# Gather conditions kept to one engine, and the tables of extra blocks moved into the first expert of a mixture-of-experts kernel

## The chip, the cores and the metric

The kernel runs on one core of one Trainium2 chip. The metric is the device time of one launch in microseconds. The kernel before takes 1557.82 us, the median of three runs (1555.93 to 1558.26).

Five engines work side by side, each with its own queue of instructions: PE (TensorE, matrix products), DVE (VectorE), ACT (ScalarE), POOL (GpSimd) and SP (SyncE, which here does little but issue transfers). Waits between them are semaphores. An engine's queue is in order: whatever stands behind a waiting instruction waits too.

## The reference

One decoder block over 512 tokens of width 1024, and after it a mixture of experts. The experts are where the change lies, so only they are shown:

```
def moe(h, router_w, router_b, w_in, b_in, w_out, b_out):
    logits = (tok @ router_w + router_b)            # tok: 512 x 1024, 32 experts
    top_val, top_idx = lax.top_k(logits, TOP_K)     # TOP_K = 4
    weights = jax.nn.softmax(top_val, axis=-1)
    ...                                             # tokens sorted by expert, padded to blocks
    def expert_block(args):
        rows, e = args
        xb = tok[rows]
        gu = xb @ w_in[e] + b_in[e]                 # 1024 x 2048
        gate, up = gu[:, :D_EXPERT], gu[:, D_EXPERT:]
        gate = jnp.minimum(gate, SWIGLU_LIMIT)
        up = jnp.clip(up, -SWIGLU_LIMIT, SWIGLU_LIMIT)
        act = (up + 1) * (gate * jax.nn.sigmoid(SWIGLU_ALPHA * gate))
        return act @ w_out[e] + b_out[e]            # 1024 x 1024
    ...                                             # weighted, added to the token's row
x = x + gate2[:, None, :] * moe(h, ...)
return rms_norm(x, final_g)
```

All weights are fp32: 12 MB for each of the 32 experts.

## The kernel before, in words

**Stages.** Up to about 400 us of the profile run the front of the block, the router and the tables that say which token goes into which slot. From 421.7 us to about 1522 us the 32 experts run one after the other. A last norm ends the kernel.

**Slots.** Each expert has a main block of slots (`ab_up` L1298, `ab_down` L1313). Where an expert got more tokens, a *single* block and a *pair* block are computed as well, each under a condition at run time: `tc.If(single[e] > 0)` and `tc.If(pair[e] > 0)`, in L1414 and L1416 for the first product ("up") and in L1437 and L1439 for the second ("down"). The up conditions stand ahead of the main `ab_up`. A condition is a branch on every engine that has work in it, and its false path still brings the semaphores to the count that the block would have left, so that others can wait on plain numbers. The two flags of an expert are loaded into a register of each engine by `values_load` in `gather_first`.

**Gathers.** POOL gathers the rows of a block from DRAM (`gather`, L1241). The gathers of single and pair blocks stand under two more conditions (L1254, L1256), which before are branches on all five engines though only POOL has work in them. They run two experts ahead.

**Tables.** `tables` (L1184) makes from sums of slots the rows to gather. The table of main blocks (`tab0`) is made in the router. Those of single and pair blocks (`tab1`, `tabp`) are made by `later_tables(1)` ahead of expert 0: 16 products with one-hots (`spread`, L1112), a copy by ACT (`slt`), five products with `reps` (L1192) and eleven operations of DVE. Then comes a condition on `most` (L1396) for the tables of the seventh block on, which is false with these inputs.

**Weights.** Each expert has 12 tiles of 1 MB: eight `wi` (L937) and four `wo` (L942). SP issues them ahead through `prefetch`. They lie in a ring of 19 places (`big`, tag "H"). Two of these are held by the one-hots `oh` and by `rx` until the tables are made. I number the tiles W0 to W11 (expert 0), W12 to W23 (expert 1) and so on. W12 to W15 go into places that are free by then. W16 goes into the place of W0, which is expert 0's `wi[0]`, W17 into that of W1, and so on: a tile is issued when the last instruction of the program that reads its predecessor is done, whether that stands in a condition or not.

**Order.** PE's order is the order in which the code is written (`manual_schedule`); the other engines' is set by the scheduler of the framework. In `ab_up` 30 of 32 products run (60 of 64 rows of the profile, which shows each as two), then `between()` (here `before_last`: `swiglu` of the first half, its transposes, the biases of the second product), then the last four. In `ab_out` `halfway` prepares the next expert's rows.

Of the kernel before, what the change touches and what calls it, by code (L numbers as in the profile page):

```python
# [9 lines left out]
F32 = mybir.dt.float32  # L10
# [31 lines left out]
def tile_hybrid_block(ctx: ExitStack, tc: tile.TileContext, x, c, ada_w, ada_b, norm1_g, w_in,  # L42
# [1049 lines left out]
    def one_hots(p_, n, i):  # L1092

        ns = slice(4 * i, 4 * i + 4)
        return v.tensor_tensor(oh[:, ns, 0:n], iota_l[:, 0:n].unsqueeze(1).to_broadcast([128, 4, n]),
                               p_[:, ns].unsqueeze(2).to_broadcast([128, 4, n]), op=OP.is_equal)
# [13 lines left out]
    def spread(t, n, i):  # L1110
        for k in range(4 * i, 4 * i + 4):
            pe.matmul(t[0:n, 0:96], oh[:, k, 0:n], rv[:, k].rearrange("p a e -> p (a e)"),  # L1112
                      start=(k == 0), stop=(k == 15))
# [15 lines left out]
    oh = H([128, 16, 128], F32R, name="oh")  # L1129
    slot_ps = M()  # L1130
# [54 lines left out]
    def tables(t, n, reps, tab, mul, o, ps_, tile_):  # L1185

        N = tab.shape[1]
        r = tile_("slt")[0:n]
        sc.activation(r, t[0:n, 0:96], AF.Copy)
        ps = ps_()  # L1190
        for b, rep in enumerate(reps):
            pe.matmul(ps[:, 96 * b:96 * b + 96], rep[0:n], r, start=True, stop=True)  # L1192
        pv = ps[:, 0:96 * N].rearrange("p (n v e) -> p n v e", n=N, v=3)
        iv, em = [tile_(n).rearrange("p (n e) -> p n e", e=32)[:, 0:N] for n in ("iv", "em")]
# [11 lines left out]
    tables(slot_ps, 64, rep64, tab0, 2.0, 2, M, front_tile)  # L1206
# [38 lines left out]
    single, pair = {}, {}  # L1245

    def gather_first(e):
        single[e], pair[e] = [nc.values_load(nbt[0:1, o + e:o + e + 1], min_val=0, max_val=1) for o in (32, 64)]  # L1248
# [110 lines left out]
    for t in xab[1:] + xce:  # L1359
        gp.memset(t, 0.0)  # L1360

# [12 lines left out]
    def later_tables(ch):  # L1374
# [6 lines left out]
        s_ = rows_of(0) if ch == 1 else None  # L1381
        tab = mo.tile([128, 512], F32, tag="yab", bufs=2, name="tl")[:, 0:384].bitcast(I32) if ch > 1 else None
        tab = tab.rearrange("p (n e w) -> p n e w", n=4, w=3) if ch > 1 else tab1
        tables(t, 128, rep32, tab, 4.0, 0, PT, mo_tile)
        if ch == 1:
            tables(t, 64, rep64, tabp, 2.0, 2, PT, mo_tile)
            v.copy_predicated(tab1[:, 0], pair4.unsqueeze(2).to_broadcast([128, 32, 3]), tab1[:, 2])
        gp.dma_start(tabl[4 * ch - 2:4 * ch + 2].rearrange("n p f -> p n f"), tab.rearrange("p n e w -> p n (e w)"))
        return s_
# [16 lines left out]
    def expert(e, xT, sel, p):  # L1406
        (wi, wo), n = W[e], e // 16
        x_ = xce[e % 3]
        if e + 2 < NE:
            gather_first(e + 2)  # L1410
            gather_more(e + 2)
        sel1 = selectors(e + 1) if e + 1 < NE else None
        act, last = acts(2, "act"), acts(3, "actc")
        with tc.If(single[e] > 0):  # L1414
            c_up(transposed(x_[:, 512:768], 2, "xc", 2, True), wi, sel, n, last[2])
        with tc.If(pair[e] > 0):  # L1416
            pp = [PC(), PC()]
            xp = transposed(x_[:, 0:512], 4, "xab", 2, True)
            ab_up(xp, wi, up_biases(sel, n, pp))
            for t, a_ in zip(pp, last):  # L1420
                swiglu(t, a_)
# [14 lines left out]
        swiglu(p[1], act[1])  # L1436
        with tc.If(single[e] > 0):  # L1437
# [38 lines left out]

    with tc.If(most > 5):
# [91 lines left out]
```

## Time and profile before

| | us |
|---|---|
| median of three runs | 1557.82 |
| the profiled execution's own time | 1551.44 |
| its span (first to last instruction) | 1549.9 |
| PE busy in it | 1388.0 (90%) |
| time before and behind the span | 1.5 |

The profile is one execution, 6.4 us below the median. In the rows, "x" is a count, times are from the span's start, and what stands in brackets is the idle time of the engine just before, with what ended it. PEq, SPq and DVEq are the sequencers of these engines: time that went into branches, loads of registers or semaphores.

### The profile page before, as it was taken

To read this page: it belongs to the slowest core of one execution; us is meant where nothing else is said; L and a number is where in the kernel's file an instruction comes from. 1 tells how busy PE (TensorE), PEld (TensorE's weight loads), DVE (VectorE), ACT (ScalarE), POOL (GpSimd) and SP (SyncE) were. 2 spreads that over 40 slices of the span, in tenths; PEclk is the share of its full clock that TensorE was granted. 3 is DMA by queue.
4 is the path that set the end of the run, shared out by engine and by line. 5 is a ranking of instruction groups with operands and counts; after the bars stand their busy time and mean duration, and the time that the engine had idled before them with its cause. 6 is when DMAs were issued, how large, how long until landed. Compare 5 with 4: busy or idle time off the path is not lost. (4 is left out here: it accounts for less than half of the span.)

```text
span 1549.9 us, 22296 instructions
## 1 busy us (share of the span) xinstructions
PE 1388.0 (90%) x7895; PEld 673.5 (43%) x7896; DVE 451.5 (29%) x1089; ACT 346.1 (22%) x830; POOL 220.4 (14%) x181
## 2 busy tenths in 40 slices
PE   5759999999588889999999999999999999998992
PEld 4548877778433333333333333333333333333330
DVE  7558932474411111111111111112112111111113
ACT  3452333334211211121120111111121111221112
POOL 3733100000200110111010110111101111110001
PEclk9879999999599999999999999999999999999997
DMA  9424576594799999999997899999999999678953
GB/s 313 135 63 136 214 256 179 170 342 156 286 391 407 410 405 404 405 407 400 408 402 280 330 398 409 406 353 398 402 409 372 399 411 405 246 292 332 388 181 131
DMA packets 128918, 497.11 MB, mean 321 GB/s; under 512 B 23588, under 2 KB 31236, under 8 KB 95972
## 3 DMA queue, kind: packets, MB, share of 16 engines
q1 hardware_dynamic: 113844, 468.50, 77.2%
q0 software_dynamic: 11888, 20.84, 5.9%
q10 hardware_dynamic: 3008, 5.38, 1.0%
q8 instruction: 114, 1.87, 0.5%
q14 instruction: 64, 0.52, 0.1%
HBM read 476.75 MB, written 20.40 MB: 321 GB/s over the span
## 5 line engine op out<-in xcount | busy, mean ns | idle before, releaser
L1304 PE MATMUL pu<-wi,xab 128*64 128x512 f32 x2048 | 463.0, 604 | 42.2 <-PEq L1416 33.2
L1304 PEld LDWEIGHTS pu<-wi,xab 128*64 128x64 f32 x2048 | 165.1, 139 | 315.3 <-issue 304.5
L1317 PE MATMUL pd<-wo,aab 128*64 128x512 f32 x1024 | 234.6, 598 | 16.9 <-PEq L1439 15.5
L1279 ACT ACTIVATE s<-g 128x256 f32<-128x256 f32 x88 | 36.6, 416 | 679.8 <-DVE g L1278 669.1
L1317 PEld LDWEIGHTS pd<-wo,aab 128*64 128x64 f32 x1024 | 74.5, 137 | 155.8 <-issue 141.3
L1278 DVE TENSOR_SCALAR g<-pu 128x256 f32<-128x256 f32 x64 | 27.0, 421 | 354.0 <-PE pu L1304 353.7
L1270 ACT ACTIVATE xab<-pt,sh2c,g2c 128x64 f32<-128x64 f32 x304 | 93.8, 413 | 11.1 <-PE pt L1264 9.4
L1338 PE MATMUL pc<-wi,xc 128*32 128x512 f32 x768 | 85.1, 594 | 3.1 <-ACT xc L1270 2.9
L1304 PE MATMUL pc<-wi,xab 128*64 128x512 f32 x384 | 83.9, 594 | 2.2 <-DMA wi<-in_moe_w_in 1.3
L1326 DVE SCALAR_TENSOR_TENSOR yab<-pd,tab,gate2h 128x512 f32<-128x512 f32 x32 | 24.0, 751 | 200.4 <-PE pd L1317 200.4
L1241 POOL DMA_INDIRECT xab<-hrow,tab x32 | 34.2, 1070 | 327.7 <-PE pt L1264 325.6
L1355 POOL DMA_INDIRECT acc<-yab,tab x32 | 51.1, 1597 | 159.4 <-DVE yab L1326 71.1
L1355 POOL DMA_INDIRECT acc<-yc,tab x12 | 19.9, 1657 | 350.8 <-DVEq L1439 232.8
L174 ACT ACTIVATE whi<-wraw 128x1024 fp32r<-128x1024 f32 x46 | 48.2, 1056 | 90.5 <-PE g L386 65.0
L386 PE MATMUL g<-hhi,whi 128*128 128x512 f32 x160 | 64.6, 404 | 1.8 <-ACT hhi L498 1.8
L386 PE MATMUL g<-hlo,whi 128*128 128x512 f32 x160 | 63.8, 399 | 1.5 <-DVE hlo L492 1.4
L386 PE MATMUL g<-hhi,wlo 128*128 128x512 f32 x160 | 63.5, 397 | 0.0
L1272 ACT ACTIVATE aab<-pt 128x256 f32<-128x256 f32 x64 | 24.5, 383 | 149.2 <-PE pt L1264 149.2
L1278 DVE TENSOR_SCALAR g<-pc 128x256 f32<-128x256 f32 x24 | 10.2, 424 | 162.4 <-PE pc L1338 86.7
L175 POOL TENSOR_TENSOR wlo<-wraw,whi 128x1024 fp32r<-128x1024 f32 x16 | 40.5, 2535 | 89.5 <-ACT whi L174 89.0
L1304 PEld LDWEIGHTS pc<-wi,xab 128*64 128x64 f32 x384 | 27.3, 137 | 56.2 <-issue 50.9
L1338 PEld LDWEIGHTS pc<-wi,xc 128*32 128x32 f32 x768 | 23.6, 110 | 57.4 <-issue 40.1
(442 smaller groups left out, 1616.4 us busy)
## 6 DMA issues: line engine op xcount, KB each, us to landing
wi<-in_moe_w_in SPq DMA_DIRECT2D x256, 1024.0 KB, 17.0
wo<-in_moe_w_out SPq DMA_DIRECT2D x128, 1024.0 KB, 14.2
adaw<-in_ada_w SPq DMA_DIRECT2D x16, 1024.0 KB, 5.2
wraw<-in_w_in SPq DMA_DIRECT2D x12, 1024.0 KB, 7.4
wraw<-in_ada_w SPq DMA_DIRECT2D x8, 1024.0 KB, 9.3
wraw<-in_w_out SPq DMA_DIRECT2D x4, 1024.0 KB, 9.8
xt<-in_x SPq DMA_DIRECT2D x4, 512.0 KB, 5.3
wraw<-in_w_in SPq DMA_DIRECT2D x4, 512.0 KB, 13.4
```

Of the source, the lines that this page charges most:

```text
L174: sc.activation(dst_hi, src, AF.Copy)
L175: lo.tensor_sub(dst_lo, src, dst_hi)
L386: pe.matmul(P["ps"][m], l, r, start=(k == 0 and n == 0), stop=(k == 2 * P["n"] - 1 and n == 2))
L1241: gp.indirect_dma_start(out=dst, out_offset=None, in_=rows_, in_offset=bass.IndirectOffsetOnAxis(ap=idx, axis=0), bounds_check=n * S - 1, ...
L1270: sc.activation(t[:, o:o + w], ps[:, o:o + w], AF.Identity, scale=g2c[:, k:k + 1], bias=sh2c[:, k:k + 1])
L1272: sc.activation(t, ps[:, 0:128 * n], AF.Copy)
L1278: v.tensor_scalar(g, p[:, 0:256], LIMIT, None, op0=OP.min)
L1279: sc.activation(sg, g, AF.Sigmoid, scale=ALPHA)
L1304: pe.matmul(p[u][64 * g:64 * g + 64, :].rearrange("p (a b) -> p a b", a=2), xT[:, k % 4, 64 * (k // 4):64 * (k // 4) + 64], wi[k][:, :, 51 ...
L1317: pe.matmul(p[64 * g:64 * g + 64, :], aT[:, k % 2, 16 * (k - k % 4):16 * (k - k % 4) + 64], wo[k // 2 + j][:, k % 2, 512 * g:512 * g + 512 ...
L1338: pe.matmul(p[32 * g:32 * g + 32, :].rearrange("p (a b) -> p a b", a=2), xT[:, k % 2, 32 * (k // 2):32 * (k // 2) + 32], wi[k][:, :, 256 * ...
L1355: gp.indirect_dma_start(out=rows_, out_offset=bass.IndirectOffsetOnAxis(ap=icol, axis=0), in_=y, in_offset=None, compute_op=OP.add)
```

## The change

- The flags of an expert are loaded twice: for POOL alone in `gather_more`, and for PE, DVE, ACT and POOL in `halfway` of the expert before (for expert 0 ahead of it). The gather conditions are branches of POOL alone; SP, PE, ACT and DVE keep an unconditional branch for each. SP loads no flags.
- `later_tables` is split: `later_sums` (spreads and the ACT copy) stays ahead of expert 0; the products with `reps` and DVE's table operations are moved into expert 0's `before_last`. The gathers that need these tables are moved there too.
- In expert 0 alone the up conditions (`more_up`, now L1427 and L1429) stand behind the main `ab_up` and its `swiglu`, since their tables are made within it. In the other experts they stay ahead.
- `rx` is stored to DRAM (`rvd`, a transfer of POOL's), and the condition on `most` with the tables of the seventh block on is moved behind the last expert, where `oh` and `rv` are built anew.
- POOL's order is now as written, too; `xab[1]` is cleared and gathered before the other clears; the transposes of expert 0's rows come behind the sums.

```
-    ordered = tc.manual_schedule(engines={ET.PE})
+    ordered = tc.manual_schedule(engines={ET.PE, ET.Pool})
     ordered.__enter__()
-    xT0 = later_tables(1)
+    slots1 = later_sums(1)
+    xT0 = rows_of(0)
     sel0 = selectors(0)
-    most = nc.values_load(nbt[0:1, 96:97], min_val=0, max_val=NBMAX)
-    with tc.If(most > 6):
-        for ch in (2, 3, 4):
-            later_tables(ch)
-    gather_more(0)
-    gather_first(1)
-    gather_more(1)
+    single[0], pair[0] = flags(0, MAIN)
...
+    MAIN = [ET.PE, ET.DVE, ET.Activation, ET.Pool]
...
+    def flags(e, engines):
+        return [nc.values_load(nbt[0:1, o + e:o + e + 1], engines, min_val=0, max_val=1,
+                               skip_runtime_bounds_check_because="a comparison's result, 0 or 1") for o in (32, 64)]
+
     def gather_more(e):
         x_ = xce[e % 3]
-        with tc.If(single[e] > 0):
+        s1, p1 = flags(e, [ET.Pool])
+        with tc.If(s1 > 0):
             gather(x_[:, 512:768], hrow4, tab1[:, 0, e, 0:1], 4)
-        with tc.If(pair[e] > 0):
+        with tc.If(p1 > 0):
             gather(x_[:, 0:512], hrow2, tabp[:, 0, e, 0:1], 2)
...
     gather_first(0)
-    for t in xab[1:] + xce:
+    gp.memset(xab[1], 0.0)
+    gather_first(1)
+    for t in xab[2:] + xce:
         gp.memset(t, 0.0)
+    gp.dma_start(rvd, rv.bitcast(F32))
...
+        if e:
+            gathers()
+            more_up()
         aT, nxt = [], []
         def before_last():
+            if e == 0:
+                later_tables(1, slots1)
+                gather_more(0)
+                gather_more(1)
+                gathers()
             swiglu(p[0], act[0])
...
         def halfway():
             aT1 = transposed(act[1], 2, "aab", 2)
             if sel1 is not None:
+                single[e + 1], pair[e + 1] = flags(e + 1, MAIN)
                 nxt.extend((rows_of(e + 1), sel1, main_sums(e + 1, sel1)))
             return aT1
         ab_up(xT, wi, p, before_last)
         swiglu(p[1], act[1])
+        if e == 0:
+            more_up()
...
+    most = nc.values_load(nbt[0:1, 96:97], min_val=0, max_val=NBMAX)
+    with tc.If(most > 6):
+        hot[:] = H([128, 16, 128], F32R, name="oh"), H([128, 16, 3, 32], F32R, name="rv")
+        rvf = H([128, 16, 3, 32], name="rvf")
+        nc.sync.dma_start(rvf, rvd)
+        sc.activation(hot[1], rvf, AF.Copy)
+        for ch in (2, 3, 4):
+            later_tables(ch, later_sums(ch))
```

**PE around expert 0.** PE's queue before, from the two up conditions of expert 0 to the end of its main up product (`pu`); `pc` are products of the conditional blocks:

```order
L1414 COMPARE_AND_BRANCH
L1264 MATMUL pt<-ident,xce_3337 128x128 x2
L1287 MATMUL pc<-bhl,sel 128x512
L1338 MATMUL pc<-wi,xc 32x512 x32
L1414 UNCONDITIONAL_BRANCH x2
L1416 COMPARE_AND_BRANCH
L1264 MATMUL pt<-ident,xce_3337 128x128 x4
L1287 MATMUL pc<-bhl,sel 128x512 x2
L1304 MATMUL pc<-wi,xab 64x512 x32
L1416 UNCONDITIONAL_BRANCH x2
L1304 MATMUL pu<-wi,xab 64x512 x30
```

And PE's queue now, from the last matrix products of the main up product ahead of the tables to the end of the pair condition:

```order
L1314 MATMUL pu<-wi,xab 64x512 x30
L1197 MATMUL pt<-slt,reps 128x96 x5
...
L1274 MATMUL pt<-ident,act 128x128 x2
L1297 MATMUL pd<-bhl,sel 128x256 x2
L1314 MATMUL pu<-wi,xab 64x512 x2
L1427 COMPARE_AND_BRANCH
...
L1348 MATMUL pc<-wi,xc 32x512 x32
L1427 UNCONDITIONAL_BRANCH x2
L1429 COMPARE_AND_BRANCH
...
L1314 MATMUL pc<-wi,xab 64x512 x32
L1429 UNCONDITIONAL_BRANCH x2
```

Before, the main products of expert 0 are the last readers of its `wi` tiles; now the products in the pair condition are, and they stand behind the main ones.

**SP at the tiles W14 to W19.** SP's queue before, from W14 on (bracketed are the semaphores that an issue waits for):

```order
L937 DMA wi<-in_moe_w_in 128x2048 [waits PE_49]
...
L937 DMA wi<-in_moe_w_in 128x2048 [waits DVE_49]
L937 DMA wi<-in_moe_w_in 128x2048 [waits DMAHW7_49,PE_49]
L937 DMA wi<-in_moe_w_in 128x2048 [waits PE_49]
L942 DMA wo<-in_moe_w_out 128x2x1024 [waits DMAHW1_49,PE_49]
```

SP's queue now, from W14 on:

```order
L937 DMA wi<-in_moe_w_in 128x2048 [waits DVE_49,PE_49]
L937 DMA wi<-in_moe_w_in 128x2048 [waits DMASW6_49]
L1503 TENSOR_LOAD nbt [waits DVE_49]
...
L1462 UNCONDITIONAL_BRANCH
L937 DMA wi<-in_moe_w_in 128x2048 [waits DMAHW7_49,PE_49]
L1464 UNCONDITIONAL_BRANCH
L937 DMA wi<-in_moe_w_in 128x2048 [waits PE_49]
L942 DMA wo<-in_moe_w_out 128x2x1024 [waits DMAHW1_49]
```

In both pieces the row that waits for DMAHW7 and PE is W16, the two rows behind it (branches apart) are W17 and W18, and W14 and W15 stand ahead of it. W16's count of PE's semaphore is now one that is reached only at the pair condition of expert 0, inside it or on its false path. W18 waits for no PE any more, since W17 ahead of it does.

**DVE behind the one-hots.** DVE's queue before, from the one-hots to the end of the tables, and then what follows; here without the rows of `tabp`, which lie ahead of the load:

```order
L1095 TENSOR_TENSOR oh<-rc,pos_2782 128x512 x3
L1364 TENSOR_SCALAR sel<-qsel,esel 128x384 x2
L1195 TENSOR_SCALAR em<-pt 128x128 [waits PE_49]
L1196 TENSOR_SCALAR iv<-pt,offs 128x128
L1197 SCALAR_TENSOR_TENSOR tab_3286<-em,iv 128x128 [waits DVE_49]
...
L1395 TENSOR_LOAD nbt [waits DVE_49]
L1396 COMPARE_AND_BRANCH
```

DVE's queue now, from the first `sel` to the first half's `swiglu` (`g`, `u`):

```order
L1377 TENSOR_SCALAR sel<-qsel,esel 128x384
L1095 TENSOR_TENSOR oh<-rc,pos_2782 128x512 [waits DVE_49]
L1095 TENSOR_TENSOR oh<-rc,pos_2782 128x512 x3
L1377 TENSOR_SCALAR sel<-qsel,esel 128x384
L1200 TENSOR_SCALAR em<-pt 128x128 [waits PE_49]
...
L1206 TENSOR_TENSOR tabp<-tabp,pt 128x32 [waits Activation_49]
L1288 TENSOR_SCALAR g<-pu 128x256 [waits DVE_49]
L1290 TENSOR_SCALAR u<-pu 128x256
```

One `sel` has moved ahead of the one-hots, and the tables stand directly ahead of the first half's `swiglu` in expert 0.

## Rows read from the trace of the kernel before

**Rows 1.** The page, parts 1 and 2: PE's busy time; GB/s in 40 slices.

```profile
PE 1388.0 (90%) x7895; PEld 673.5 (43%) x7896; DVE 451.5 (29%) x1089; ACT 346.1 (22%) x830; POOL 220.4 (14%) x181
GB/s 313 135 63 136 214 256 179 170 342 156 286 391 407 410 405 404 405 407 400 408 402 280 330 398 409 406 353 398 402 409 372 399 411 405 246 292 332 388 181 131
```

**Rows 2.** Waits of PE, 410 to 1550 us: total, times, longest.

```profile
PE pu L1304 <- PEq L1416: 33.2, 24, 4.3
PE pu L1304 <- DMA wi<-in_moe_w_in: 4.6, 1, 4.6
...
PE pc L1304 <- DMA wi<-in_moe_w_in: 1.3, 1, 1.3
```

**Rows 3.** Stretches: length, busy PE PEld DVE ACT POOL (count), PEclk, DMA share, GB/s.

```profile
426.00:766.00 340.00, 306.32 (x1632) 116.06 (x1630) 53.37 (x125) 57.69 (x171) 41.57 (x32) 0.98 1.02 404
436.50:438.50 2.00, 1.45 (x8) 0.67 (x8) 0.40 (x1) 0.38 (x1) 0.00 (x0) 1.00 0.92 217
...
814.00:853.00 39.00, 38.63 (x231) 14.26 (x229) 7.03 (x17) 3.07 (x8) 2.29 (x2) 1.00 0.71 275
```

**Rows 4.** Timeline of PE at 765 us, in expert 11's pair block.

```profile
765.20 4.51 PE L1304 MATMUL pc<-wi,xab 128*64 128x512 f32 x20 [1.29 <-DMA wi<-in_moe_w_in]
```

**Rows 5.** Timeline of SP: issues of W12 to W17; W16 and W17 alone.

```profile
408.56 18.66 SPq L937 DMA_DIRECT2D wi<-in_moe_w_in  x6
...
425.17 2.04 SPq L937 DMA_DIRECT2D wi<-in_moe_w_in  x2
```

**Rows 6.** Timeline of PE around expert 0.

```profile
409.26 1.10 PE L1264 MATMUL pt<-ident,xab 128*128 128x128 f32 x4
412.96 1.47 PE L1192 MATMUL pt<-slt,reps 128*128 128x96 f32 x5 [2.61 <-ACT xab L1270]
417.47 1.22 PE L1287 MATMUL pu<-bhl,sel 128*128 128x512 f32 x2 [3.04 <-DVEq L1396]
421.74 14.56 PE L1304 MATMUL pu<-wi,xab 128*64 128x512 f32 x60 [3.05 <-PEq L1416]
437.05 0.41 PE L1264 MATMUL pt<-ident,act 128*128 128x128 f32 x2 [0.75 <-DVEq L1437]
...
439.44 3.65 PE L1317 MATMUL pd<-wo,aab 128*64 128x512 f32 x16 [0.73 <-PEq L1439]
...
452.55 14.52 PE L1304 MATMUL pu<-wi,xab 128*64 128x512 f32 x60 [4.60 <-DMA wi<-in_moe_w_in]
```

**Rows 7.** Timeline of POOL; indirect DMAs issued 400 to 480 us, median us to landing.

```profile
405.16 1.60 POOL L1241 DMA_INDIRECT xab<-hrow,tab  x1 [1.31 <-DVE pos L1106]
...
acc<-yab,tab POOLq DMA_INDIRECT x2, 9.9
...
xce<-hrow,tab POOLq DMA_INDIRECT x1, 7.1
```

**Rows 8.** Timelines of DVE and ACT around expert 0.

```profile
407.47 2.44 DVE L1364 TENSOR_SCALAR sel<-qsel,esel 128x384 fp32r<-128x384 f32 x2
414.09 0.29 DVE L1195 TENSOR_SCALAR em<-pt 128x128 f32<-128x128 f32 x1 [4.18 <-PE pt L1192]
416.06 0.19 DVE L1201 TENSOR_TENSOR tabp<-tabp,pt 128x32 f32<-128x32 f32 x1
436.48 0.42 DVE L1282 SCALAR_TENSOR_TENSOR act<-u,g 128x256 f32<-128x256 f32 x1
...
410.44 2.47 ACT L1270 ACTIVATE xab<-pt,sh2c,g2c 128x64 f32<-128x64 f32 x8 [0.70 <-PE pt L1264]
415.81 0.21 ACT L1200 ACTIVATE tabp<-pt 128x32 f32<-128x32 f32 x1 [0.74 <-DVE iv L1196]
434.27 1.28 ACT L1279 ACT_TABLE_LOAD   x1 [18.25 <-DVE g L1278]
```

**Rows 9.** Timeline of PE later: main up products behind a single block, and behind none.

```profile
867.58 13.10 PE L1304 MATMUL pu<-wi,xab 128*64 128x512 f32 x60 [0.33 <-PEq L1416]
...
896.37 13.10 PE L1304 MATMUL pu<-wi,xab 128*64 128x512 f32 x60 [0.73 <-PEq L1416]
```

More of the change, by code (lines that the diff above doesn't have):

```diff
@@ L1129, in tile_hybrid_block @@
     oh = H([128, 16, 128], F32R, name="oh")
+    hot = [oh, rv]
+    rvd = dram.tile([128, 16, 3, 32], F32, name="rvd")
     slot_ps = M()
@@ L1184, in tile_hybrid_block, with sums, tables @@
     pair4 = rt.tile([128, 32], mybir.dt.uint8, name="pair4")
-    def tables(t, n, reps, tab, mul, o, ps_, tile_):
+    def sums(t, n, tile_):
+        r = tile_("slt")
+        sc.activation(r[0:n], t[0:n, 0:96], AF.Copy)
+        return r
+    def tables(r, n, reps, tab, mul, o, ps_, tile_):
         N = tab.shape[1]
-        r = tile_("slt")[0:n]
-        sc.activation(r, t[0:n, 0:96], AF.Copy)
         ps = ps_()
         for b, rep in enumerate(reps):
-            pe.matmul(ps[:, 96 * b:96 * b + 96], rep[0:n], r, start=True, stop=True)
+            pe.matmul(ps[:, 96 * b:96 * b + 96], rep[0:n], r[0:n], start=True, stop=True)
         pv = ps[:, 0:96 * N].rearrange("p (n v e) -> p n v e", n=N, v=3)
-        iv, em = [tile_(n).rearrange("p (n e) -> p n e", e=32)[:, 0:N] for n in ("iv", "em")]
+        iv, em = [tile_(m).rearrange("p (n e) -> p n e", e=32)[:, 0:N] for m in ("iv", "em")]
         v.tensor_scalar(em, pv[:, :, 0], 0.0, None, op0=OP.is_equal)
@@ L1204, in front_tile @@
         return sm.tile([128, 96], F32R, name=n) if n == "slt" else sm.tile([128, 64], F32, name=n)
-    tables(slot_ps, 64, rep64, tab0, 2.0, 2, M, front_tile)
+    tables(sums(slot_ps, 64, front_tile), 64, rep64, tab0, 2.0, 2, M, front_tile)
     cps = M()
@@ L1245, in tile_hybrid_block @@
     single, pair = {}, {}
+    MAIN = [ET.PE, ET.DVE, ET.Activation, ET.Pool]
     def gather_first(e):
-        single[e], pair[e] = [nc.values_load(nbt[0:1, o + e:o + e + 1], min_val=0, max_val=1) for o in (32, 64)]
         gather(xab[e % 3], hrow2, tab0[:, 0, e, 0:1], 2)
+    def flags(e, engines):
+        return [nc.values_load(nbt[0:1, o + e:o + e + 1], engines, min_val=0, max_val=1,
+                               skip_runtime_bounds_check_because="a comparison's result, 0 or 1") for o in (32, 64)]
     def gather_more(e):
         x_ = xce[e % 3]
-        with tc.If(single[e] > 0):
+        s1, p1 = flags(e, [ET.Pool])
+        with tc.If(s1 > 0):
             gather(x_[:, 512:768], hrow4, tab1[:, 0, e, 0:1], 4)
-        with tc.If(pair[e] > 0):
+        with tc.If(p1 > 0):
             gather(x_[:, 0:512], hrow2, tabp[:, 0, e, 0:1], 2)
@@ L1372, in main_sums, with later_sums @@
         return up_biases(sel, e // 16, [pab.tile([128, 512], F32, tag=f"pu{u}", name="pu") for u in range(2)])
-    def later_tables(ch):
+    def later_sums(ch):
         t = PT()
@@ L1380, in later_tables @@
             spread(t, 128, i)
-        s_ = rows_of(0) if ch == 1 else None
+        return sums(t, 128, mo_tile)
+    def later_tables(ch, r):
         tab = mo.tile([128, 512], F32, tag="yab", bufs=2, name="tl")[:, 0:384].bitcast(I32) if ch > 1 else None
         tab = tab.rearrange("p (n e w) -> p n e w", n=4, w=3) if ch > 1 else tab1
-        tables(t, 128, rep32, tab, 4.0, 0, PT, mo_tile)
+        tables(r, 128, rep32, tab, 4.0, 0, PT, mo_tile)
         if ch == 1:
-            tables(t, 64, rep64, tabp, 2.0, 2, PT, mo_tile)
+            tables(r, 64, rep64, tabp, 2.0, 2, PT, mo_tile)
             v.copy_predicated(tab1[:, 0], pair4.unsqueeze(2).to_broadcast([128, 32, 3]), tab1[:, 2])
         gp.dma_start(tabl[4 * ch - 2:4 * ch + 2].rearrange("n p f -> p n f"), tab.rearrange("p n e w -> p n (e w)"))
-        return s_
-    ordered = tc.manual_schedule(engines={ET.PE})
+    ordered = tc.manual_schedule(engines={ET.PE, ET.Pool})
     ordered.__enter__()
-    xT0 = later_tables(1)
+    slots1 = later_sums(1)
+    xT0 = rows_of(0)
     sel0 = selectors(0)
-    most = nc.values_load(nbt[0:1, 96:97], min_val=0, max_val=NBMAX)
-    with tc.If(most > 6):
-        for ch in (2, 3, 4):
-            later_tables(ch)
-    gather_more(0)
-    gather_first(1)
-    gather_more(1)
+    single[0], pair[0] = flags(0, MAIN)
     first = dram.tile([1, 96], I32, name="first")
@@ L1408, in expert, with gathers, more_up @@
         x_ = xce[e % 3]
-        if e + 2 < NE:
-            gather_first(e + 2)
-            gather_more(e + 2)
         sel1 = selectors(e + 1) if e + 1 < NE else None
         act, last = acts(2, "act"), acts(3, "actc")
[L1414 to L1421, printed above, removed]
+        def gathers():
+            if e + 2 < NE:
+                gather_first(e + 2)
+                gather_more(e + 2)
+        def more_up():
+            with tc.If(single[e] > 0):
+                c_up(transposed(x_[:, 512:768], 2, "xc", 2, True), wi, sel, n, last[2])
+            with tc.If(pair[e] > 0):
+                pp = [PC(), PC()]
+                xp = transposed(x_[:, 0:512], 4, "xab", 2, True)
+                ab_up(xp, wi, up_biases(sel, n, pp))
+                for t, a_ in zip(pp, last):
+                    swiglu(t, a_)
+        if e:
+            gathers()
+            more_up()
         aT, nxt = [], []
         def before_last():
+            if e == 0:
[3 more added lines that the diff above has]
+                gathers()
             swiglu(p[0], act[0])
```

4 lines of the change are left out of this document (2 added, 2 removed).

## The prediction, as made before the changed kernel had run

> **What bounds the kernel now.** I read the page first. PE is busy for 1388.0 us, 90% of the span, and the row of GB/s stands near 405 for slices on end [rows 1]. So two resources are close to full, and the question is which one sets the end in which stretch. The waits of PE say little for DMA: over all experts PE waits for weights once for 4.6 us and once for 1.3 us, against 33.2 us in 24 waits for the sequencer at the up conditions [rows 2]. The stretches say more. From 426 to 766 us the DMA share is 1.02 at 404 GB/s, without a hole; only behind 814 us does it fall, to 0.71 [rows 3]. At 765.20 us, in expert 11's pair block, PE waits 1.29 us for the last `wi` tile of that expert, W139 [rows 4]. PE had run ahead of the stream's needs until then, but here it has no lead left. So the time at 765 us is set by when the stream of weights starts for good, and by its rate. Behind it, from 814 us, the share of 0.71 shows a stream that waits for places that PE frees [rows 3], so there PE sets the time, and a delay at 765 us is carried to the end.
>
> When does the stream start? SP issues W12 to W17 between 408.56 and 427.2 us; W16, the first tile into a place of expert 0's, goes out at 425.17 [rows 5], when PE, which began the main up product at 421.74 [rows 6], is done with W0. From W16 to W139 are 124 tiles; 765.20 - 425.17 = 340.0 us is 2.74 us for each, at a share of 1.02 [rows 3]. One hole is in it: at 436.5 to 438.5 us the stream moves 217 GB/s instead of 404, which costs 2 x (1 - 217/404) = 0.9 us [rows 3].
>
> **The change, part by part.** The step that decides is W16. After the change the pair condition is the last reader of expert 0's `wi` tiles, and it stands behind the main up product and its `swiglu`. W16 therefore goes out when PE has passed both conditions, and W17 to W23 right behind it. When is that?
>
> - Start of the main up product. The transposes of expert 0's rows need the gather, issued at 405.16 [rows 7], and the sums' products, which wait for the one-hots. One `sel` now comes ahead of these; two took 2.44 us [rows 8], so +1.2, and the transposes, at 409.26 before [rows 6], could run at 410.5. The gather now runs beside W12 and W13, since SP has no flags to wait for. I give it the 7.1 us of the slower kind of gather [rows 7]: it lands at 412.3. ACT begins scaling 1.18 us behind the start of the transposes, and the first of eight pieces takes about 0.41 [rows 6, 8]: 413.9. The biases fit beneath ACT. Bounds: no delay at all, 409.26 + 1.18 + 0.41 = 410.9; a landing as slow as the 9.9 us of a scatter [rows 7], 416.7.
> - 60 rows of `ab_up`: 14.56 us [rows 6]; at best 13.10, as in a later expert [rows 9]. 428.5.
> - Five `reps` products, now on PE's path: 1.47 us before [rows 6], at half the clock at worst and so half of it at best, 0.74; I take 0.8 since PE has just worked. 429.3.
> - DVE's eleven table operations, ahead of `swiglu`: from 414.09 to 416.06 + 0.19 = 416.25, 2.16 us [rows 8]. 431.4. Before, they lay ahead of expert 0, on the path as well.
> - `swiglu` of the first half. ACT's last table copy ends 0.23 us ahead of DVE's last operation, and ACT's table load of 1.28 us [rows 8] then starts at once, since it now waits for nothing else: 1.05 past DVE's end. From the load's end to the end of `act` were 436.90 - 435.55 = 1.35 us [rows 8]: 2.4 in all. Bounds: 1.75 without the load, 3.1 with the load behind `g` as before. 433.8.
> - Transposes, biases and the last four rows: from `act`'s end at 436.90 to 439.44 - 0.73 = 438.71, 1.81 us [rows 6, 8]. 435.7.
> - The two conditions, both false: 0.73 us [rows 9]; 0.33 for one alone, and 3.05 at worst, as at expert 0 before [rows 6]. 436.4.
>
> So W16 goes out at 436.4 instead of 425.17: 11.2 us later. The hole of 0.9 us at 437 goes, since eight tiles are queued at once. That leaves +10.3 us for W139's landing, and PE has no slack for it. Bounds: all low ends, 410.9 + 13.10 + 0.74 + 2.16 + 1.75 + 1.81 + 0.33 = 430.8, with the hole taken off +4.7; all high ends, 416.7 + 14.56 + 1.47 + 2.16 + 3.1 + 1.81 + 3.05 = 442.8, the hole kept, +17.7.
>
> A rule bears on the last step. The waits at the conditions run from 0.33 and 0.73 us [rows 9] to 4.60 right behind the start of the full stream [rows 6]. The Trainium skill ("Runtime: NRT & Kernel Launch", Instruction fetch mechanics) says that a taken branch to a target outside the window of fetched instructions has to fetch by DMA first. The trace agrees as far as it goes: the 4.60 us stand where the stream is full, the 0.33 to 0.73 us in the steady run. By that rule the step costs what the fetch makes of it, and with 3.05 instead of 0.73 the sum would be 2.3 us higher.
>
> The other parts I cost at nothing:
> - Gather conditions and flag loads off PE, ACT, DVE and SP. Between experts PE's sequencer is ahead of the array, so these ran beneath products. The gap of 0.73 us ahead of a plain expert's main up product becomes 0.33 when the single block ran [rows 9], so it is made by the up conditions, which stay. Bounds: 0 and 0.4 us in 24 waits, 9.6 us.
> - Flags now loaded in `halfway`: beneath the 16 rows of the second product (3.65 us each time) [rows 6]. Without that cover, some tenths for each expert.
> - One condition more at the end of the program: at most about 1 us, beside the last scatter. The store of `rx` holds POOL's queue, ahead of the clears and gathers, and W15; its cost is within the bound of the gather.
> - Expert 0's earlier start on PE. PE reaches the second product at 436.4 instead of 439.44; this only adds to the lead that the stream eats up.
>
> Against the profiled run's own time: 1551.44 + 10.3 = 1561.7 us. The median of the runs shown stands 6.4 above that execution, and nothing in the change touches the reason: 1557.82 + 10.3 = 1568.1 us.
>
> A second rule weighs on the gather. In the listing, gathers and scatters take 7.1 to 9.9 us beside weights [rows 7]. The Trainium skill ("DMA: Bandwidth & Descriptors", Queues, rings and completion order) has each DMA engine go round its queues packet by packet. The trace doesn't contradict it, but no row here shows a gather with an empty stream to set against it. By that rule and the 9.9 us the sum would be 2.8 us higher; without any delay, 3.0 lower.
>
> **Rivals.**
> - *PE bounds from the start (faster).* Place: expert 0. If W16 is not held back (its release comes with the main product's first rows), the early start counts: 3.1 us at the second product, and up to 3.9 of the 4.60 us ahead of expert 1, 7.0 in all: 1550.8 us. For it: DMA waits of 5.9 us in all [rows 2]. Against: the order of PE and SP, and the wait at 765.20 [rows 4]. It decides from a W16 that goes out before 426 us. Chance 0.06.
> - *The late stream is absorbed (same).* The lead of PE would have to be larger at 765 us than it is, or the stream would have to run faster later. For it: PE waits only 1.29 us there. Against: the share of 1.02 [rows 3]. It gives 1556 to 1560 us. Chance 0.09.
> - *The removed branches count in each expert.* 0.4 us in 24 waits, 9.6 us; alone 1548.2 us; the two thirds of it behind 765 us together with the late stream +3.9, 1561.7. Against: [rows 9]. Chance 0.04 for the case alone; the mixture lies within the range.
> - *It does not do what it says:* flags wait for a transfer or an engine. Then some tenths for each expert come on top of the late stream; within the range.
>
> **How the numbers follow.** Chance 0.81 for the late stream. Its own range is 1562.5 (+4.7) to 1575.5 (+17.7). Reaching into the case "same", the range is 1559 to 1575.5. What cannot be told from no change is 0.2%, 3.1 us. Slower by more: 0.81, and 0.02 from "same": 0.83. Within: 0.07 and a little of the others, 0.08. Faster: 0.06 and 0.03: 0.09.
>
> **What would show it.** W16's issue at about 436 us in SP's timeline, behind the pair condition, and an empty stream ahead of it for about ten us; expert 0's main up product at about 414 us; the gap ahead of the transposes of `act` at about 5 us; PE waiting for `wi` from about expert 8 on, with the wait in expert 11's pair block near 775 us; gaps between plain experts still near 0.73 us. I am wrong if W16 goes out before 430 us, if PE waits for no weights ahead of expert 11, or if the gaps between experts shrink.

## The result, and the profile after

The changed kernel takes 1582.72 us (median of four runs, 1577.6 to 1587.77), the kernel before 1558.04 (1555.93 to 1561.69): a ratio of 1.0161, 95% interval 1.0138 to 1.0184. It is slower by 24.7 us. The direction and the mechanism came out as forecast; the size did not: 10.3 us were forecast, and 1582.72 lies above the range, which ended at 1575.5.

One correction first. The prediction numbered the tiles two too low: SP had issued W12 and W13 already at 393.82 us, so the first tile into a place of expert 0's, which it calls W16, is W18. All times in it stand; only the name was off (and from W18 to W139 are 122 tiles, 2.79 us each). Below it is W18, or the first released tile.

The profiled run of the changed kernel took 1580.2 us, 28.8 more than that of before. Its page, against [rows 1]:

```profile
PE 1399.3 (89%) x7895; PEld 669.4 (42%) x7896; DVE 451.6 (29%) x1089; ACT 346.5 (22%) x829; POOL 222.7 (14%) x182
GB/s 313 111 78 134 210 256 183 156 359 153 266 300 409 401 405 410 406 402 412 401 407 233 298 406 402 407 355 388 407 402 356 383 408 388 303 219 347 399 213 129
```

The page hardly tells the two apart; the stretches do. Four of them, with the columns of [rows 3]: ahead of W18, the full stream, a piece of it at expert 9, and behind it:

```profile
426.00:443.50 17.50, 12.30 (x53) 4.35 (x49) 4.31 (x17) 2.75 (x6) 1.88 (x2) 0.87 0.05 13
444.00:782.00 338.00, 294.39 (x1540) 107.39 (x1542) 51.04 (x119) 55.20 (x167) 40.54 (x31) 0.94 1.02 405
709.00:726.00 17.00, 9.08 (x32) 2.10 (x30) 1.60 (x4) 0.42 (x1) 0.00 (x0) 0.51 1.02 416
792.00:850.00 58.00, 56.53 (x299) 19.50 (x297) 10.90 (x27) 11.14 (x34) 4.27 (x3) 1.00 0.78 308
```

For 17.5 us the DMA engines move next to nothing (share 0.05), where before they were full from 426 us on. Then the stream runs at the same share of 1.02, and at 405 GB/s against 404 in [rows 3]. SP's timeline has the start, against 425.17 in [rows 5]:

```profile
443.59 0.82 SPq L937 DMA_DIRECT2D wi<-in_moe_w_in  x2
```

PE around expert 0, against [rows 6]:

```profile
418.72 1.08 PE L1274 MATMUL pt<-ident,xab 128*128 128x128 f32 x4 [4.34 <-DMA xab<-hrow,tab]
419.71 1.19 PE L1297 MATMUL pu<-bhl,sel 128*128 128x512 f32 x2
420.83 13.65 PE L1314 MATMUL pu<-wi,xab 128*64 128x512 f32 x60
434.42 0.89 PE L1197 MATMUL pt<-slt,reps 128*128 128x96 f32 x5
439.83 0.66 PE L1274 MATMUL pt<-ident,act 128*128 128x128 f32 x2 [4.53 <-DVE act L1292]
...
440.85 1.98 PE L1314 MATMUL pu<-wi,xab 128*64 128x512 f32 x4
447.39 6.28 PE L1327 MATMUL pd<-wo,aab 128*64 128x512 f32 x16 [4.57 <-PEq L1464]
...
459.38 13.10 PE L1314 MATMUL pu<-wi,xab 128*64 128x512 f32 x60 [0.84 <-PEq L1429]
```

The last four rows of the main product end at 442.83, and W18 goes out 0.76 us behind them: it waits for both conditions, as forecast. (The row at 439.83 shows that PE stood still for 4.53 us ahead of them; over the last four the granted clock is 0.50, 1.2 GHz, the lower of its two levels.) POOL ahead of it, against [rows 7], and DVE and ACT, against [rows 8]:

```profile
406.42 0.62 POOL L1373 DMA_DIRECT2D rvd<-rx  x1 [102.35 <-DVE rx L1089]
...
409.88 3.94 POOL L1246 DMA_INDIRECT xab<-hrow,tab  x1 [1.36 <-DVE pos L1106]
```

```profile
435.10 0.29 DVE L1200 TENSOR_SCALAR em<-pt 128x128 f32<-128x128 f32 x1 [22.30 <-PE pt L1197]
437.08 0.19 DVE L1206 TENSOR_TENSOR tabp<-tabp,pt 128x32 f32<-128x32 f32 x1
439.26 0.42 DVE L1292 SCALAR_TENSOR_TENSOR act<-u,g 128x256 f32<-128x256 f32 x1
...
437.06 1.28 ACT L1289 ACT_TABLE_LOAD   x1
```

From the first table operation to the end of `act` are 439.68 - 435.10 = 4.58 us; 4.56 were forecast. Then PE's timeline where it meets the stream: two rows of expert 4 (one of five waits in its single block, and the main product behind them), then expert 9's single block and the main products of experts 9 and 10:

```profile
542.70 1.94 PE L1348 MATMUL pc<-wi,xc 128*32 128x512 f32 x8 [1.98 <-DMA wi<-in_moe_w_in]
...
554.02 13.62 PE L1314 MATMUL pu<-wi,xab 128*64 128x512 f32 x60 [0.32 <-PEq L1429]
...
700.70 3.64 PE L1348 MATMUL pc<-wi,xc 128*32 128x512 f32 x32 [0.24 <-ACT xc L1280]
704.94 1.07 PE L1348 MATMUL pc<-wi,xc 128*32 128x512 f32 x8 [0.60 <-DMA wi<-in_moe_w_in]
708.00 1.28 PE L1348 MATMUL pc<-wi,xc 128*32 128x512 f32 x8 [1.99 <-DMA wi<-in_moe_w_in]
711.75 1.94 PE L1348 MATMUL pc<-wi,xc 128*32 128x512 f32 x8 [2.46 <-DMA wi<-in_moe_w_in]
714.86 1.93 PE L1348 MATMUL pc<-wi,xc 128*32 128x512 f32 x8 [1.17 <-DMA wi<-in_moe_w_in]
721.07 15.41 PE L1314 MATMUL pu<-wi,xab 128*64 128x512 f32 x60 [4.28 <-PEq L1429]
...
753.98 13.10 PE L1314 MATMUL pu<-wi,xab 128*64 128x512 f32 x60 [2.54 <-issue]
```

In [rows 4] PE met the stream in expert 11 and lost 1.29 us. Now it meets it in expert 4, with five waits of 6.67 us in all, and again in expert 9, with four of 6.22 us. Behind the waits of expert 9 come three costs that the forecast did not have: the condition takes 4.28 us instead of 0.33, the main product 15.41 instead of 13.10 (eight products cost 1.94 instead of 1.07; the granted clock in 709 to 726 is 0.51, just above 1.2 GHz), and the next expert starts 2.54 us late. In expert 11's pair block there is no wait left.

The waits alone do not make the condition dear: behind those of expert 4 it took 0.32 us. What stands in the 4.28 us, from 716.8 to 721.07, is a packet of instructions (a row of the DMA queues: packets, MB, share):

```profile
q8 instruction: 1, 0.02, 1.5%
```

It runs from 718.24 to 719.26, and PE goes on 1.81 us behind its end. From the end of the last products to 554.02, in expert 4, there is none. The kernel before has such conditions too, with such a packet in each, but in experts 2 and 3, where PE still had a lead to lose:

```profile
482.27 14.79 PE L1304 MATMUL pu<-wi,xab 128*64 128x512 f32 x60 [4.35 <-PEq L1416]
...
512.05 15.48 PE L1304 MATMUL pu<-wi,xab 128*64 128x512 f32 x60 [4.12 <-PEq L1416]
```

Over the run, against [rows 2]:

```profile
PE pu L1314 <- PEq L1429: 29.3, 23, 4.3
...
PE pc L1348 <- DMA wi<-in_moe_w_in: 12.9, 9, 2.5
PE pt L1274 <- DVE act L1292: 4.5, 1, 4.5
```

In sum the conditions ahead of the main products cost no more than before, 29.3 against 33.2 us. What is new is that two dear ones stand behind the last wait for weights, where nothing covers them.

And the gap between plain experts is what it was in [rows 9], 0.73 us:

```profile
921.38 13.10 PE L1314 MATMUL pu<-wi,xab 128*64 128x512 f32 x60 [0.73 <-PEq L1429]
```

### The profile page after: what moved, and what is told of

Same layout as the page of the kernel before. It is cut to its first block, busy times and chain, and to the rows that moved or that the text cites. A ratio compares the mean times of both kernels' runs of the same rounds, so it can differ in the third digit from the quotient of the medians.

```text
span 1578.6 us, 21656 instructions
## 1 busy us (share of the span) xinstructions
PE 1399.3 (89%) x7895; PEld 669.4 (42%) x7896; DVE 451.6 (29%) x1089; ACT 346.5 (22%) x829; POOL 222.7 (14%) x182
## 5 line engine op out<-in xcount | busy, mean ns | idle before, releaser
L1314 PE MATMUL pu<-wi,xab 128*64 128x512 f32 x2048 | 461.5, 603 | 33.2 <-PEq L1429 29.3
L1314 PEld LDWEIGHTS pu<-wi,xab 128*64 128x64 f32 x2048 | 161.6, 139 | 309.2 <-issue 299.6
L1289 ACT ACTIVATE s<-g 128x256 f32<-128x256 f32 x88 | 36.7, 417 | 690.7 <-DVE g L1288 690.7
L1348 PE MATMUL pc<-wi,xc 128*32 128x512 f32 x768 | 92.2, 624 | 15.8 <-DMA wi<-in_moe_w_in 12.9
L1274 PEld LDWEIGHTS pt<-ident,act 128*128 128x128 f32 x176 | 17.9, 142 | 70.7 <-issue 61.0
```

Of the source, the lines that this page charges most:

```text
L1289: sc.activation(sg, g, AF.Sigmoid, scale=ALPHA)
L1314: pe.matmul(p[u][64 * g:64 * g + 64, :].rearrange("p (a b) -> p a b", a=2), xT[:, k % 4, 64 * (k // 4):64 * (k // 4) + 64], wi[k][:, :, 51 ...
L1348: pe.matmul(p[32 * g:32 * g + 32, :].rearrange("p (a b) -> p a b", a=2), xT[:, k % 2, 32 * (k // 2):32 * (k // 2) + 32], wi[k][:, :, 256 * ...
```

## The experiments

My theory after the result: the late first tile is the loss, and nothing else in the change is of that size. The rival: the loss sits in the parts that stay when that is undone (slower gather, store of `rx`, flags in each expert, tables inside expert 0).

**a1: expert 0's conditions and tables ahead again, the rest of the change kept.**

```
+    later_tables(1, slots1)
     sel0 = selectors(0)
+    gather_more(0)
+    gather_more(1)
...
-        if e: gathers(); more_up()
+        gathers(); more_up()
```

> The changed kernel with one part undone: the tables of extra blocks and the two up conditions of expert 0 stand ahead of its main product again; flags, gather conditions on GpSimd alone and the tables of the seventh block at the end stay. Theory (the weight stream restarts late because the pair condition is the last reader of expert 0's tiles): W16 goes out about 3.5 us behind the start of expert 0's main product, near 424 us, and the time falls back to 1552 to 1560 us. Rival (the loss sits in the parts that stay: the slower gather, the store of rx, flags in each expert): it stays above 1572 us.

Measured: 1559.85 us, ratio 1.0012 (0.9989 to 1.0034). No loss is left that can be told from none. The first released tile is back:

```profile
428.47 2.48 SPq L937 DMA_DIRECT2D wi<-in_moe_w_in  x2
```

**a2: the changed kernel without expert 0's conditional blocks.**

```
-        if e == 0:
-            more_up()
-        with tc.If(single[e] > 0): ...    # and pair
+        if e:
+            with tc.If(single[e] > 0): ...
```

> The changed kernel without expert 0's four conditional blocks (none of them is taken with these inputs); the tables stay inside expert 0. Only the release of W16 to W23 differs. Theory (late stream): W16 near 424.5 us, the stream runs from there, 1554 to 1562 us, although PE still waits some 4.5 us for the tables in expert 0. Rival (the tables' stall on PE in expert 0 and the slow gather are the loss): above 1572 us.

Measured: 1561.07 us, 1.0015 (0.9998 to 1.0032). PE still waits for the tables in expert 0, yet the time is back. PE's row and SP's:

```profile
443.92 0.66 PE L1274 MATMUL pt<-ident,act 128*128 128x128 f32 x2 [4.52 <-DVE act L1292]
```

```profile
427.47 2.04 SPq L937 DMA_DIRECT2D wi<-in_moe_w_in  x2
```

So 4.5 us of an idle PE in expert 0 cost nothing that can be seen, while the tile's 16 us cost nearly all.

**a3: tables ahead, conditions still behind.** Only the tables' place is undone (`later_tables(1, slots1)` ahead of `sel0`, `more_up` as in the changed kernel).

> The changed kernel with the tables ahead of expert 0 again, but with its up conditions still behind the main product. Theory (late stream): W16 still goes out only behind the pair condition, near 440 to 444 us, and the time stays at 1576 to 1586 us. Rival (the tables' place is the loss): 1555 to 1565 us.

Measured: 1573.14 us, 1.0081 (1.0052 to 1.0110), below the expected band though its profiled run took 1582.76. W18 went out at 441.42. The release alone gives half to two thirds of the loss in these runs; the rest is not told apart by this one.

**b1: the kernel before, with only expert 0's up conditions moved behind its main product.**

```
+        if e:
+            more_up()
...
         swiglu(p[1], act[1])
+        if e == 0:
+            more_up()
```

> The kernel before with one part of the change alone: expert 0's up conditions moved behind its main product and swiglu. Theory (late stream): W16 near 439.5 us instead of 425.2, 14 us later; PE meets the stream two experts earlier and pays for it in branches and clock as well, 14 to 24 us: 1572 to 1582 us. Rival (the loss sits in flags, gathers, tables or the front): no change, 1555 to 1561 us.

Measured: 1576.22 us, 1.0107 (1.0077 to 1.0137). One move of code, without flags, gathers, tables or store, makes about two thirds of the loss (1.07% against 1.61%). W18 at 446.20, 38.1 us behind the front's last product. Its expert 9 is worth a look beside the one above:

```profile
711.94 1.07 PE L1338 MATMUL pc<-wi,xc 128*32 128x512 f32 x8 [1.53 <-DMA wi<-in_moe_w_in]
715.48 1.83 PE L1338 MATMUL pc<-wi,xc 128*32 128x512 f32 x8 [2.47 <-DMA wi<-in_moe_w_in]
718.00 1.56 PE L1338 MATMUL pc<-wi,xc 128*32 128x512 f32 x8 [0.69 <-DMA wi<-in_moe_w_in]
719.88 13.10 PE L1304 MATMUL pu<-wi,xab 128*64 128x512 f32 x60 [0.33 <-PEq L1418]
```

PE came later to the stream, waited for three tiles, and the condition behind them took 0.33 us and the product 13.10. It had paid 4.17 us at a condition of expert 8, at 690.7 us, with an instruction packet in it.

**b2: the kernel before, with expert 0's up conditions in the middle of its main product** (behind 32 of 64 rows, by a second hook in `ab_up` at `(k, u) == (4, 0)`).

> The kernel before with expert 0's up conditions in the middle of its main product (behind 32 of 64 rows): W16 near 430 us instead of 425, about a third of the delay of b1. Theory (a us of delay is a us or somewhat more at the end, from the first us on): 1561 to 1566 us, between the kernel before and b1. Rival (there is slack that swallows the first us): 1556 to 1559.

Measured: 1561.80 us, 1.0023 (1.0001 to 1.0046). W18 at 430.46: 5.3 us later than before, and some 3.6 us slower by the ratio. The loss grows with the delay; how much slack there is for its first us these runs do not say, since six of the twelve lie at 1555 to 1560 us and six at 1563 to 1570.

**a4: the changed kernel with the store of `rx` behind the gather in POOL's queue.**

```
     ordered.__enter__()
+    gather_first(0)
+    gp.dma_start(rvd, rv.bitcast(F32))
```

> The changed kernel with the store of rx to DRAM moved behind expert 0's gather in GpSimd's queue (in the changed kernel it stands ahead of it). If the store is what slows the gather, PE's wait ahead of the transposes of expert 0's rows falls from 4.3 us to about 1, W16 goes out some 3 us earlier against the spreads, and the time falls by about 3 us, to 1577 to 1582. Rival (W12 and W13, issued earlier than before, slow the gather): wait and time stay.

Measured: 1577.37 us, 1.0118 (1.0098 to 1.0137). The gather's wait shrinks, not to 1 us but to 2.78:

```profile
412.73 1.09 PE L1274 MATMUL pt<-ident,xab 128*128 128x128 f32 x4 [2.78 <-DMA xab<-hrow,tab]
```

So the store is a part of it, and not all: the gather takes 6.78 us here, 8.84 in the changed kernel and at most 4.1 before. Nothing of that reaches the release. W18 goes out 36.68 us behind the front's last product, against 36.65: of 1.57 us won at the transposes 0.86 went into the biases and 0.61 into the 60 rows. So the 5.3 us by which this profile is shorter are not the store's. Its front ended 4.4 us earlier, and in expert 9, behind four waits, the condition took 0.32 us instead of 4.28 (some 3 us of the two are lost again later):

```profile
710.51 1.93 PE L1348 MATMUL pc<-wi,xc 128*32 128x512 f32 x8 [1.36 <-DMA wi<-in_moe_w_in]
712.76 14.21 PE L1314 MATMUL pu<-wi,xab 128*64 128x512 f32 x60 [0.32 <-PEq L1429]
```

An instruction packet ran here from 706.90 to 707.79, mostly beneath a wait for a tile.

**a5: a1 and a4 together.**

> Both: conditions and tables of expert 0 ahead as in a1, and the store behind the gather. Expected from a1 (1.0012 of the kernel before) less the gather's 3 us: 1552 to 1558 us, 0.997 to 1.000 of the kernel before. If the gather's delay is absorbed: as a1.

Measured: 1560.97 us, 1.0013 (0.9995 to 1.0030); no gain over a1. A miss of the main expectation; the other one, a delay that is absorbed, held.

**a7: a2 and a4 together.**

> Expert 0's conditional blocks left out (not taken with these inputs) and the store behind the gather. The stream starts as early as it can here: W16 about 3.5 us behind the main product's start, no tables ahead of it. Theory (each us of W16's issue counts): 1550 to 1557 us, below the kernel before. Rival (PE sets the time as soon as the stream is early enough): no better than a1 and a2, 1557 to 1562.

Measured: 1557.75 us, 1.0000 (0.9984 to 1.0016). W18 went out 15.8 us behind the front's last product (the one with `rep64`, L1192 before and L1197 now), against 22.9 before; nothing was won by it, and the time lies in the rival's band.

**c1: a5 with the two conditions at the end nested into one.**

```
     with tc.If(most > 5):
+        with tc.If(most > 6): ...
```

> As a5 (conditions and tables of expert 0 ahead, store behind the gather), with the condition for the tables of the seventh block put inside the one for the sixth, so that one condition stands at the end as before. If the second condition at the end is what makes the last stretch (from the last expert's main product to the end) 54.2 to 55.0 us instead of 52.7, this falls to about 52.8 and the time by 2 us against a5: 1557 to 1560, ratio 0.999 to 1.001. Rival (the stretch is longer for another reason): 54.9 us as a5.

Measured: 1558.53 us, 1.0009 (0.9993 to 1.0026); the last stretch, from the last expert's main product to the end of the run, is 54.35 us, against 54.93 in a5 and 52.71 before. The second condition makes at most 0.6 of the 2.2 us. From the last scatter's issue to the load of the sum are 6.62 us here, 6.08 in a5, 6.83 in the changed kernel, and 1528.55 - 1523.39 = 5.16 before:

```profile
1529.82 1.56 POOL L1365 DMA_INDIRECT acc<-yab,tab  x1 [22.98 <-DVE yab L1336]
```

```profile
1536.44 1.76 SPq L1521 DMA_DIRECT2D fin<-acc  x4
```

Why the load comes later there stays open.

**c4: a version meant to beat both.** As a7, but with expert 0's conditional blocks kept: they run at the end, under the one condition there, on weights loaded anew; and a small transfer of `nbt` on SP is meant to hold W14 back until the gather is under way.

> A version meant to be the fastest: no conditional blocks inside expert 0 (they are computed at the end, under the one condition that stands there, from weights loaded anew), the tables inside expert 0, the store behind the gather, W14 issued behind the gather (a small transfer of the counts holds SP), one condition at the end. Theory (each us of the first released tile's issue, against the front's end, counts at the end): that tile goes out 13 to 15 us behind the front's last product with reps, 7 us less than before, and the time is 1549 to 1556 us, 0.994 to 0.998 of the kernel before. Rival (from expert 9 on PE loses what the stream gains): 0.998 to 1.001.

Measured: 1560.63 us, 1.0004 (0.9983 to 1.0026). A miss; no version here beats the kernel before. The transfer did not hold W14 back: it went out at 411.83, ahead of the gather at 412.76, which took 8.27 us. Its W18 is out at 426.54, 18.0 us behind the front's last product, but its expert 9 has the same rows as the changed kernel's:

```profile
696.69 1.93 PE L1350 MATMUL pc<-wi,xc 128*32 128x512 f32 x8 [2.64 <-DMA wi<-in_moe_w_in]
700.48 1.93 PE L1350 MATMUL pc<-wi,xc 128*32 128x512 f32 x8 [1.85 <-DMA wi<-in_moe_w_in]
706.82 14.45 PE L1316 MATMUL pu<-wi,xab 128*64 128x512 f32 x60 [4.41 <-PEq L1432]
```

**d1: the kernel before, with only the flags and the gather conditions of the change.**

```
     def gather_more(e):
+        s1, p1 = flags(e, [ET.Pool])
...
+                single[e + 1], pair[e + 1] = flags(e + 1, MAIN)     # in halfway
```

> The kernel before with the other part of the change alone: gather conditions on GpSimd alone, GpSimd's order as written, and the flags of each expert loaded amid the second product; tables, up conditions and the tables of the seventh block stay where they were. If branches and loads were hidden beneath products: the gaps between plain experts stay at 0.73 us and the time at 1555 to 1560, ratio 0.998 to 1.001 (a us or two may come from expert 0, which no longer runs through six gather branches). If they cost in each expert: gaps of 0.33 us, about 1548 to 1552, ratio 0.994 to 0.996.

Measured: 1561.44 us, 1.0043 (1.0028 to 1.0058): slower, by 6.7 us by the ratio (the medians differ by 4.6), which neither theory had. The gaps between plain experts did not shrink. Expert 0 starts late instead:

```profile
416.07 1.09 PE L1270 MATMUL pt<-ident,xab 128*128 128x128 f32 x4 [4.66 <-DMA xab<-hrow,tab]
...
428.27 14.65 PE L1310 MATMUL pu<-wi,xab 128*64 128x512 f32 x60 [5.50 <-PEq L1423]
```

SP, without flags to wait for, issues W14 at 408.03, beside the gather at 407.84; the gather takes 8.2 us instead of 4.1 at most, and W18 goes out at 431.79, 6.6 us later than before. 1.75 of these 6.6 us are the front, 0.9 a later issue of the gather, and the rest the gather. So the loss has the same path again, by another door; that it is the gather's alone was not tried.

**The changed kernel once more**, for a second profile.

> The changed kernel unaltered, for a second profile. If the 4.7 us by which the front of the block ended later in its first profile than in that of before are chance, this front ends anywhere between 402 and 412 us; the first released tile goes out 36 to 37 us behind it in any case, and expert 9's single block is where PE first waits for weights. If the front is slower by the change, it ends at 406 to 408 again.

Measured: 1583.49 us, one run. The front's last product at 408.22, W18 at 446.26, 38.0 us behind it; expert 9's main product at 724.28, 278.0 us behind W18. Two parts of the expectation missed: the 38.0 us, and the first wait for weights, which stands in expert 4's single block, at 540.15. The late front came again.

All profiles side by side (us from the span's start; "front" is that product of 64x96):

| kernel | front | W18 out | e9 main | e11 main | profiled run | ratio |
|---|---|---|---|---|---|---|
| before | 402.23 | 425.17 | 699.52 | 769.51 | 1551.44 | 1 |
| a7 | 409.87 | 425.69 | 706.28 | 778.13 | 1559.61 | 1.0000 |
| c1 | 406.24 | 426.27 | 705.17 | 777.30 | 1559.29 | 1.0009 |
| c4 | 408.52 | 426.54 | 706.82 | 780.11 | 1564.67 | 1.0004 |
| a5 | 406.58 | 426.96 | 703.74 | 775.66 | 1561.71 | 1.0013 |
| a2 | 411.54 | 427.47 | 703.11 | 774.96 | 1559.18 | 1.0015 |
| a1 | 406.75 | 428.47 | 702.37 | 774.33 | 1559.61 | 1.0012 |
| b2 | 402.77 | 430.46 | 704.16 | 774.70 | 1560.20 | 1.0023 |
| d1 | 403.98 | 431.79 | 705.78 | 775.19 | 1558.77 | 1.0043 |
| a4 | 402.52 | 439.20 | 712.76 | 783.76 | 1574.93 | 1.0118 |
| a3 | 406.15 | 441.42 | 719.08 | 790.80 | 1582.76 | 1.0081 |
| changed | 406.94 | 443.59 | 721.07 | 793.45 | 1580.20 | 1.0161 |
| b1 | 408.08 | 446.20 | 719.88 | 789.35 | 1578.14 | 1.0107 |
| again | 408.22 | 446.26 | 724.28 | 796.86 | 1583.49 | - |

Expert 9's main product follows W18 by 273.6 to 275.6 us in seven of them, and by 276.8 to 280.6 in the other seven. What parts the two is the condition ahead of that product: 0.32 or 0.33 us in the first seven, 4.26 to 5.01 in the others.

## Why the prediction was wrong in size

**Right: the mechanism.** Release behind the pair condition, an empty stream ahead of it, an unchanged rate, PE without lead, the delay carried to the end. b1 shows it from one side (conditions behind, 1.07% slower), a1 and a2 from the other (undone, within 0.15% of before). The rival "PE bounds from the start" fell. That branches and loads are hidden is shown by the gaps (0.73 us, unchanged); none of the kernels shows a gain from them.

**The sum.** The two profiles differ by 28.8 us, and the trace says where. W18 goes out 18.4 us later; 4.7 of it is the front, which ended later in this run. It is not the change alone: kernels with the front's code of before have 402.23, 402.77 and 408.08 (before, b2, b1), and the changed one has 402.52 in a4. But in nine of ten profiles with the changed code the front ends at 406.15 us or later, and in one of four with the other; whether the change makes a late front likelier is not settled. Behind the front the release cost 13.7 us, against 11.2 forecast. From W18's issue to W139's the stream made up 3.8 us, against 0.9 for the hole. From W139's issue (743.04 and 757.68) to expert 11's main product are 26.5 us before and 35.8 now: 9.3 us, against nothing forecast. From there to the end are 4.8 us more, 1.8 of them behind the start of the last expert, against at most 1. Together 4.7 + 13.7 - 3.8 + 9.3 + 4.8 = 28.7. The medians differ by 24.7: the profiled run of before is 6.6 us below its median, that of the changed kernel 2.5.

**The step that failed** is "that leaves +10.3 us for W139's landing, and PE has no slack for it": the landing was well sized (W139 out 14.6 us later, 4.7 of them the front), but what PE itself pays behind its last wait for weights was put at nothing. In experts 9 and 10 that is 1.93 us for 1.07 in the last eight products, 4.28 for 0.33 at the condition, 15.41 for 13.10 in the main product and 2.54 for 0.73 at the next one: 9.0 us, of which 1.7 are saved again at expert 11, where the wait of before is gone. The prediction took 0.33 and 0.73 us for the conditions of the steady run, and a dear one only as a bound at expert 0. The dear ones were on record: [rows 2] has 4.3 us as the longest of 24 waits, and the 4.60 us of [rows 6], which the prediction counts once as a wait for weights and once as a condition, have an instruction packet in them as well. The Trainium skill ("Runtime: NRT & Kernel Launch", Instruction fetch mechanics) says that a taken branch out of the window of fetched instructions has to wait for a DMA fetch of its target. The trace agrees: a packet of 16 KB ends 1.81 us ahead of the product that the 4.28 us precede. So the size of the late stream was near, and the price of a branch without lead was missing.

**The terms of the release.** The gather was sized 7.1 us and took 8.84; 4.1 at most before. A4 shows the store's part, d1 that of the tiles, which fits the Trainium skill's rule that a DMA engine takes its queues in turn, packet by packet ("DMA: Bandwidth & Descriptors", Queues, rings and completion order). That the turns are what costs the gather its time no run here shows. In d1 and before, W14 goes out 0.2 and 3.4 us behind the gather's issue, and the gather takes 8.2 and at most 4.1 us. The 60 rows took 13.65 instead of 14.56, the four last 1.98 instead of 1.08, behind a PE that had stood still for 4.53 us, at a granted clock of 0.50; the biases did not fit beneath ACT, +0.5. The tables and `swiglu` came within 0.02 us. PE's earlier start on the second product, which the prediction added to the lead, did not come: with 4.57 us at a condition ahead of it, it began at 447.39 and not at 436.4.

**The flags had a side that was seen and priced too low.** SP's wait for them before had also kept W14 off the gather; the prediction had that in its 7.1 us. In d1 it makes the change's quiet half 0.43% slower by itself. Why a1, with the same flags, shows no such loss is not tried: there expert 0 no longer runs through the condition on `most`, and its main product starts 18.0 us behind the front's last product, against 24.3 in d1.

**What would have shown it:** PE's first waits for `wi` came in expert 4, at 539.65 us, sooner than "about expert 8 on" had it, and then in expert 9. The wait in expert 11 near 775 us did not come; what PE had lost at experts 9 and 10 gave the stream time to land those tiles.

Still open: how a3 and b1, which hold the tile back as long as the changed kernel does, lose only 1.0081 and 1.0107. The profiles point at the passage through expert 9 (273.7 us behind W18 in b1, 277.5 in the changed kernel) and at the end; a3 has 277.7 there like the changed kernel, and its profiled run was its slowest. With four or five runs each I can't tell more.

## What to carry to other kernels

Where weights stream through a ring, the last reader in program order releases a place, taken or not: a condition moved behind the main work holds the ring until it is passed. Look for the first transfer that waits for such a release, since in a stretch that DMA bounds, its issue sets the time of all that follows, while an idle compute engine at the same place cost nothing that could be seen here (a2). And where the lead over the stream runs out inside a program with branches, price the conditions behind the last wait one by one, by the dear rows and not by the cheap ones.

## What the hardware showed unexpectedly

- **A condition that is not taken costs PE 0.3 to 5.0 us, by whether a packet of instructions comes in it.** In the fourteen profiles, each of PE's waits of more than 1.5 us ahead of a main product from expert 1 on, those for a tile apart, ends 1.3 to 1.9 us behind the end of a 16 KB packet of the instruction queue. Where that packet starts as PE falls idle, the wait is 2.3 to 3.1 us; where it starts 1.1 to 2.3 us later, 4.0 to 5.0 (4.28 in the changed kernel's expert 9, 5.01 in a5's). The queue has 114 packets in the kernel before and in the changed one; where they fall decides what they cost.
- **PE that comes early to a full stream loses what it has won.** In a7, c1 and c4 expert 8's main product started 4.8 to 7.9 us ahead of before's, and expert 9's 5.7 to 7.3 us behind it: waits for tiles, then a condition of 4.3 to 4.4 us. Where PE waits tile by tile, the eight products go from 1.07 to 1.94 us, and the granted clock in the changed kernel is 0.51 over the 17 us. In b1, with fewer waits there, it is 0.90 over the same stretch:

```profile
709.00:726.00 17.00, 11.98 (x70) 3.35 (x64) 1.61 (x4) 0.42 (x1) 0.00 (x0) 0.90 1.03 399
```

- **The front has two speeds.** The same two operations of DVE, early in the front, took 2.09 to 2.28 us in four profiles (before, b2, d1, a4), whose front ends at 402.2 to 404.0 us, and 4.61 to 4.62 in the other ten, where it ends at 406.2 to 411.5. One kernel with the code of before, b1, is among the slow ones. What decides it is not tried here. The row of the changed kernel:

```profile
25.35 4.62 DVE L492 TENSOR_TENSOR hlo<-h,hhi 128x512 fp32r<-128x512 f32 x2
```
